# Fixed TensorE order and three runs of small matmuls per head pair, in a fused SSD and short-convolution layer

## Chip, cores and metric

One Trainium2 chip, one of its cores. The metric is the device time of one execution in microseconds (us), median of three runs: 1694.2 us for the kernel before (1693.04 to 1696.69).

## What is computed

One decoder layer over 2048 tokens with model width 1024, all in f32. The input is RMS-normalised and projected once (`h @ w_in`); two groups of heads read the projection, and their joint output goes through `w_out`, a second RMS norm, the residual, and a gated per-layer embedding. The change is in the first head group, 16 heads of 64 channels, a chunked state-space scan with chunks of 128 tokens:

```python
xd = (x * dt[..., None])                                   # per head, tokens x 64
cb = einsum("bclgn,bcsgn->bgcls", cc, bc)                  # C.B per chunk and B/C group
y_diag = einsum("bgrcls,bcsgrp->bclgrp", cb[:, :, None] * decay_in, xd)
states = einsum("bclgn,bclgrp->bcgrpn", bc, xd * decay_states[..., None])
...
y_off = einsum("bclgn,bcgrpn->bclgrp", cc, prev_states) * decay_out[..., None]
y = (y_diag + y_off) + d_skip[:, None] * x
...
yz = y_ssd * silu(z_ssd);  y_ssd = rmsnorm(yz, ssd_norm)   # RMS norm per B/C group
mix = concatenate([y_ssd, y_sc], -1) @ w_out
```

## The kernel before, in words

Channels lie on the 128 partitions, tokens along the free axis. Tokens come in two blocks `b` of 1024 (TB), eight chunks (NCH) each. A Winograd-like input projection (tiles `A_...`) fills the first 1038 us and leaves x, gates, masks' sums and so on in DRAM. Then comes the stage of the **heads**, then the output projection (`mo`) and the gate (`mg`).

In the heads' stage TensorE has two kinds of work. The large one is `os`, the short-convolution half of the output projection: `under()` (L807) yields 256 units of three 128x512 matmuls, 768 in all. The small one is the scan. Heads are handled in pairs of channel tiles `(j, j+4)`, gr 0 and gr 1, four pairs per block, eight pairs in all. For one pair, with the names that the trace shows:

- `loads` (L875): `xs`, one 128x1024 tile per gr, from `xs_d` in DRAM; three buffers.
- `transposes` (L879, "T0", "T1"): 8 transposes into a PSUM tile `px`, then VectorE makes `xd` = px times dt (L891, three buffers) and `xdd` = xd times a decay (L892).
- `decays` and `mask_load`/`mask`: the decay row `ea` (one buffer, exp on ScalarE at L902), and four masks `m` (four buffers, "m00" to "m11"), each one 512 KB broadcast load, 8 exponentials on ScalarE (L939) and one VectorE product with C.B (L942).
- `states` (L908): matmuls into `pst` (L912), then VectorE runs the recurrence over chunks into `sprev` (L926) and multiplies `ea` by C (L929).
- `offsets` (L944): matmuls of `sprev` and `ea` into two PSUM tiles `py` (L955), one per gr.
- `outputs` (L959, "out0", "out1"): matmuls of `xd` and the masks into the same `py` (L967), then on VectorE y (L970) and the gate (L971), written over `xs` and stored to `yz_d`; a square on ScalarE (L976) is summed into `ssum` by VectorE (L977).

`px`, `pst`, `py`, C.B (`pg`) and the norm's sums (`pn`, L230 in `inv_rms`) share three PSUM tiles of two banks (`pss`, L743). `os` uses two banks of its own, which ScalarE empties into `po` (L830).

A list `steps` (L1008 to L1022) names the parts in the order in which they are written, and after each step some `os` units are written, so that both are spread over each other. What TensorE in fact gets is not that order: a scheduler reorders instructions of an engine where data allow it, except for the few that `open_bank` (L217) ties together. An engine then executes its list strictly in order, and SyncE's DMA issues stand in such a list too.

Of the kernel before, what the change touches and what calls it, by code (L numbers as in the profile page):

```python
# [7 lines left out]
F32 = mybir.dt.float32  # L8
# [5 lines left out]
NOSYNC = mybir.DependencyInfo(mybir.DependencyClass.NoSync, mybir.DependencyReason.DATA)  # L14

P = 128
# [4 lines left out]
TB = 1024  # L21
# [5 lines left out]
NCH = TB // CH  # L27
# [33 lines left out]
def hybrid_kernel(ctx: ExitStack, tc: tile.TileContext, xT, pT, w_t, w_dt, w_o, w_g, w_p, cols_d, cst_d, outT):  # L61
    nc = tc.nc
    V, S, G, TE = nc.vector, nc.scalar, nc.gpsimd, nc.tensor
# [40 lines left out]
    def flat(ps):  # L104
        return ps.rearrange("p g t -> p (g t)")
# [4 lines left out]
    class Weights:  # L110
# [4 lines left out]
        def __init__(self, seq):  # L115
            self.seq, self.n, self.ready = seq, 0, []
# [9 lines left out]
        def next(self, held=0):  # L126

            self.fill(self.SLOTS - held)
            return self.ready.pop(0)
# [232 lines left out]
    with ExitStack() as st:  # L362
# [352 lines left out]
        for b, prs, order in groups:  # L715
# [16 lines left out]
            if b + 1 < NB:  # L732
# [5 lines left out]
                if n in (6, 7, 8, 9, 10):  # L738
                    next(prep, None)

    pss = ctx.enter_context(tc.tile_pool(name="pss", bufs=3, space=PSUM))  # L743
# [58 lines left out]
    with ExitStack() as st:  # L802
        t4 = st.enter_context(tc.tile_pool(name="t4", bufs=2))
# [31 lines left out]
        def heads(b):  # L835
# [34 lines left out]
            def pair(j):  # L870

                jts = (j, j + 4)
                xd, xdd, xs, gz, st = [None, None], [None, None], [None, None], [None, None], {}

                def loads(gr):  # L875
                    xs[gr] = t4.tile([P, TB], F32, tag="xs", name=f"xs_{b}{jts[gr]}", bufs=3)
                    nc.sync.dma_start(xs[gr], xs_d[b][jts[gr]])

                def transposes(gr):  # L879
                    jt = jts[gr]  # L880
                    px = flat(pss.tile([P, 2, TG], F32, tag="ssd", name=f"px_{b}{jt}"))
                    for c in range(NCH):
                        cs = slice(c * CH, (c + 1) * CH)
                        TE.transpose(px[:, cs], xs[gr][:, cs], ident)
                    xd[gr] = t4.tile([P, NCH, P], F32, tag="xd", name=f"xd_{b}{jt}", bufs=3)
                    xdd[gr] = t4.tile([P, NCH, P], F32, tag="xdd", name=f"xdd_{b}{jt}")

                    def bc(a):
                        return a[:, 2 * jt:2 * jt + 2, :].rearrange("p h c -> p c h").unsqueeze(3).to_broadcast([P, NCH, 2, 64])
                    r4 = lambda a: a.rearrange("p c (h q) -> p c h q", h=2)  # L890
                    V.tensor_tensor(r4(xd[gr]), px.rearrange("p (c h q) -> p c h q", c=NCH, h=2), bc(dts[b]), ALU.mult)  # L891
                    V.tensor_tensor(r4(xdd[gr]), r4(xd[gr]), bc(dst[b]), ALU.mult)  # L892
# [86 lines left out]
                def both(*fs):  # L979
                    return lambda: [f() for f in fs]  # L980

                ml = lambda *gh: lambda: mask_load(*gh)
                mk = lambda *gh: lambda: mask(*gh)
                return {"xs0": lambda: loads(0), "xs1": lambda: loads(1), "T0": lambda: transposes(0), "T1": lambda: transposes(1), "decays": decays,
                        "load0": both(decays_load, ml(0, 0), ml(0, 1)), "load1": both(ml(1, 0), ml(1, 1)),
                        "gz0": lambda: gates_load(0), "gz1": lambda: gates_load(1),
# [9 lines left out]
        steps = []  # L996
        no = lambda: None
        pairs, norms, begins, gs = [], [], [], []
        for b in range(NB):
# [5 lines left out]
        NJ = len(pairs) // NB  # L1005
        both = lambda *fs: lambda: [f() for f in fs]
        p = pairs[0]
        steps += [both(begins[0], p["xs0"], p["xs1"], p["load0"], p["load1"]), gs[0][0], gs[0][1], p["T0"],  # L1008
                  both(p["gz0"], p["gz1"]), p["decays"], p["T1"], no, p["m00"], no]
        for n, p in enumerate(pairs):  # L1010
            b, j = divmod(n, NJ)
            q = pairs[n + 1] if n + 1 < len(pairs) else dict.fromkeys(p, no)
            fresh = j == NJ - 1 and b + 1 < NB
            steps += [both(p["states"], q["xs0"]), p["m01"], p["m10"], p["m11"], p["offsets"], p["out0"]]
            steps += [both(q["load0"], begins[b + 1]) if fresh else q["load0"], q["T0"], both(q["decays"], q["xs1"])]
            if fresh:

                steps += [p["out1"], q["load1"], norms[b], gs[b + 1][0], gs[b + 1][1], both(q["T1"], q["gz0"], q["gz1"]), no,
                          q["m00"], no]
            else:  # L1020
                steps += [p["out1"], both(q["load1"], q["gz0"]), both(q["T1"], q["gz1"]), q["m00"], no]
        steps += [norms[-1]]  # L1022

        filler = under()
        units, lead = 0, 22
# [182 lines left out]
```

## Time and profile before

| | |
|---|---|
| median of the runs | 1694.2 us (1693.04 to 1696.69) |
| the profiled execution | 1696.41 us, its span 1694.7 us |
| TensorE busy | 1658.7 us, 98% of the span |
| VectorE, ScalarE, GpSimd busy | 1255.4, 783.5, 45.6 us |
| mean granted TensorE clock | 0.996 of full speed |
| DMA | 262.27 MB, mean 155 GB/s |

How to read it: one execution is profiled, and its time (1696.41 us) is 1.7 us above its span. The trace has two records for each f32 matmul of the scan (64 where the program lists 32 offsets; one each for `os`, `mo` and the transposes). Matmul records are pipelined, each starts before the one ahead has ended, so what a run of matmuls costs is read from its first start to the start of what follows. "Idle before" names what an engine waited for. A half granted clock (0.50) makes a matmul last twice as long.

### The profile page before, as it was taken

The numbers are of one execution on the slowest core, as the hardware profiler recorded it, in microseconds if no ns is written. First come the engines' busy times: TensorE is split into PE (matmuls) and PEld (weight loads), VectorE is DVE, ScalarE is ACT, GpSimd is POOL, SyncE is SP. The second block draws the span as 40 slices with busy tenths as digits, with TensorE's granted clock in tenths as the row PEclk, the third lists the DMA queues.
The fourth block names the chain that finished last, engine by engine and source line by source line (L and its number), as shares of the span: only waits on it lengthen the run. The fifth ranks groups of instructions, "written<-read, shape, count | busy, mean of one in ns | idle before, by whom it ended". The sixth has DMA issues, their size and how long they took to land.

```text
span 1694.7 us, 22635 instructions
## 1 busy us (share of the span) xinstructions
PE 1658.7 (98%) x8324; PEld 1351.9 (80%) x8324; DVE 1255.4 (74%) x1843; ACT 783.5 (46%) x1408; POOL 45.6 (3%) x79
## 2 busy tenths in 40 slices
PE   7999999999999999999999999999999899999998
PEld 5788888888888888888888888778777677788886
DVE  7997777988669867677777685689678748878632
ACT  7763444434337434343444353666575324252421
POOL 0000000000000100100000000000000000000000
PEclk9999999999999999999999999999999999999999
DMA  9462221773226322222222237789887735636422
GB/s 303 162 211 70 97 96 61 257 251 120 69 68 213 130 80 95 78 76 68 106 82 102 73 117 239 245 277 278 261 314 242 243 100 168 197 102 211 149 95 87
DMA packets 122691, 262.27 MB, mean 155 GB/s; under 512 B 17098, under 2 KB 19658, under 8 KB 121556
## 3 DMA queue, kind: packets, MB, share of 16 engines
q1 hardware_dynamic: 122580, 260.83, 46.4%
q8 instruction: 65, 1.06, 0.2%
q14 instruction: 46, 0.38, 0.1%
HBM read 192.45 MB, written 68.33 MB: 154 GB/s over the span
## 4 chain that ended last, share of the span: by engine, by line
PE 85%; DMA 6%; DVE 6%; ACT 2%; issue 1%; SPq 0%; DVEq 0%; ACTq 0%
PE mg L214 10%; PE mo L214 8%; PE os L826 6%; PE py L967 1%; PE A_xs1X L310 1%; PE A_gc6X L310 1%; PE A_gc7X L310 1%; PE A_gb6X L310 1%; PE A_z3X L310 1%; PE A_xs3X L310 1%; PE A_gc5X L310 1%; PE A_z2X L310 1%; PE A_xs2X L310 1%; PE A_gb4X L310 1%; PE A_gc4X L310 1%; PE A_gc3X L310 1%
## 5 line engine op out<-in xcount | busy, mean ns | idle before, releaser
L826 PE MATMUL os<-act_m,ws_os 128*128 128x512 f32 x768 | 186.0, 396 | 2.4 <-ACT po L830 1.7
L214 PE MATMUL mo<-act_m,ws_o 128*128 128x512 f32 x768 | 180.9, 396 | 4.3 <-DVE x L1060 4.3
L214 PEld LDWEIGHTS mo<-act_m,ws_o 128*128 128x128 f32 x768 | 144.1, 189 | 42.1 <-issue 6.1
L214 PE MATMUL mg<-act_x2s,ws_g 128*128 128x512 f32 x768 | 176.8, 391 | 0.7 <-ACT gth L1104 0.7
L826 PEld LDWEIGHTS os<-act_m,ws_os 128*128 128x128 f32 x768 | 141.2, 188 | 37.6 <-issue 6.6
L214 PEld LDWEIGHTS mg<-act_x2s,ws_g 128*128 128x128 f32 x768 | 143.0, 188 | 34.2 <-ACT gth L1104 4.4
L139 DVE TENSOR_TENSOR ws_A_gb<-wr_A_gb,ws_A_gb 128x512 fp32r<-128x512 f32 x96 | 65.8, 686 | 33.0 <-ACT ws_A_gb L138 32.9
L138 ACT CAST ws_A_gc<-wr_A_gc 128x512 fp32r<-128x512 f32 x96 | 59.7, 622 | 57.7 <-PE A_gc5X L310 8.3
L138 ACT CAST ws_A_gb<-wr_A_gb 128x512 fp32r<-128x512 f32 x96 | 59.7, 621 | 51.6 <-PE A_cb0Y L310 4.3
L604 DVE SCALAR_TENSOR_TENSOR xo<-ux,cols,xo 128x1024 f32<-128x1024 f32 x60 | 76.7, 1280 | 6.7 <-ACT xo L600 5.6
L939 ACT ACTIVATE m<-m,adt 128x128 f32<-128x128 f32 x256 | 77.5, 391 | 0.6 <-DMA m<-acs_d 0.5
L139 DVE TENSOR_TENSOR ws_A_gc<-wr_A_gc,ws_A_gc 128x512 fp32r<-128x512 f32 x96 | 66.0, 687 | 14.1 <-ACT ws_A_gc L138 12.8
L1105 DVE SCALAR_TENSOR_TENSOR gth<-gth,pe 128x512 f32<-128x512 f32 x32 | 22.1, 691 | 70.5 <-ACT gth L1104 70.4
L1104 ACT ACTIVATE gth<-mg 128x512 f32<-128x512 f32 x32 | 19.1, 598 | 103.7 <-PE mg L214 103.6
L214 PE MATMUL A_ple<-act_p,ws_p 128*128 128x512 f32 x192 | 48.2, 409 | 9.0 <-ACT ws_p L138 8.1
L942 DVE SCALAR_TENSOR_TENSOR m<-m,gsb 128x1024 f32<-128x1024 f32 x32 | 39.6, 1246 | 19.1 <-ACT m L939 16.8
L214 PEld LDWEIGHTS A_ple<-act_p,ws_p 128*128 128x128 f32 x192 | 37.4, 196 | 18.7 <-ACT ws_p L138 9.0
L139 DVE TENSOR_TENSOR ws_A_z<-wr_A_z,ws_A_z 128x512 fp32r<-128x512 f32 x48 | 32.9, 685 | 25.2 <-ACT ws_A_z L138 25.2
L203 ACT CAST act_m<-mraw 128x512 fp32r<-128x512 f32 x64 | 38.1, 621 | 28.9 <-DVE mraw L785 15.8
L138 ACT CAST ws_A_xs<-wr_A_xs 128x512 fp32r<-128x512 f32 x48 | 29.9, 623 | 44.3 <-issue 11.6
L138 ACT CAST ws_A_z<-wr_A_z 128x512 fp32r<-128x512 f32 x48 | 29.9, 623 | 41.9 <-DVE wr_A_z L187 8.6
L1060 DVE TENSOR_TENSOR x<-mo,part 128x512 f32<-128x512 f32 x32 | 22.0, 686 | 29.3 <-PE mo L214 29.3
(499 smaller groups left out, 3597.7 us busy)
## 6 DMA issues: line engine op xcount, KB each, us to landing
wr_A_gc<-in_w_t_dram SPq DMA_DIRECT2D x64, 256.0 KB, 2.5
wr_A_gb<-in_w_t_dram SPq DMA_DIRECT2D x64, 256.0 KB, 2.8
m<-acs_d SPq DMA_DIRECT2D x32, 512.0 KB, 7.7
ple_d<-A_pe SPq DMA_DIRECT2D x32, 256.0 KB, 5.1
wr_A_xs<-in_w_t_dram SPq DMA_DIRECT2D x32, 256.0 KB, 2.6
ysc_d<-vs SPq DMA_DIRECT2D x16, 512.0 KB, 2.7
wr_A_z<-in_w_t_dram SPq DMA_DIRECT2D x32, 256.0 KB, 3.0
xs_d<-xo SPq DMA_DIRECT2D x16, 512.0 KB, 4.0
```

Of the source, the lines that this page charges most:

```text
L138: S.copy(sp[:, 0, :kn, :], raw[:, :kn, :])
L139: V.tensor_tensor(sp[:, 1, :kn, :], raw[:, :kn, :], sp[:, 0, :kn, :].bitcast(F32), ALU.subtract)
L203: S.copy(a[:, 0, :], src)
L214: TE.matmul(out, sp[:, a, (k0 + k) % 4, :], act[k0 + k][:, b, :], start=k0 + k == 0 and q == 0, stop=k0 + k == n - 1 and q == 2)
L310: TE.matmul(out, sp[:, a, k % 4, :], t[:, b, ts_], start=p in OPENS and k == 0 and q == 0, stop=k == nk - 1 and q == 2, skip_group_check=True)
L604: V.scalar_tensor_tensor(o, u[:, q:q + TB], col(w0 + q), o, ALU.mult, ALU.add)
L826: TE.matmul(ps, sp[:, a, k, :], acts_o[tg][KD + kk][:, b_, :], start=kk == 0 and n == 0, stop=kk == KD - 1 and n == 2)
L939: S.activation(m[:, c, :], m[:, c, :], AF.Exp, bias=nacs[b][:, h, c:c + 1])
L942: V.scalar_tensor_tensor(mf, mf, 1.0, s["gsb"][gr], ALU.min, ALU.mult)
L1060: V.tensor_tensor(x2[d], ps[:, i, :], pt[:, i, :], ALU.add)
L1104: S.activation(th, ps, AF.Tanh, scale=0.5)
L1105: V.scalar_tensor_tensor(th, th, 1.0, pe, ALU.add, ALU.mult)
```

## The change

From the heads on, every TensorE instruction is tied to the one written before it (class `InOrder`, a dependency without a semaphore), so that TensorE executes them as they are written. The list of steps is written anew: out0 and out1 stand directly behind the offsets, T0 and T1 of the next pair stand together, both `xs` loads of the next pair stand at the pair's states, and at the end two empty steps stand ahead of the last norm. `xs` has four buffers in place of three, `xd` two (the pool's own number) in place of three. No operation is added or left out.

```diff
+    class InOrder:
+        def __init__(self, engine):
+            self.engine, self.last = engine, None
+        def __getattr__(self, name):
+            f = getattr(self.engine, name)
+            def call(*a, **k):
+                inst = f(*a, **k)
+                if self.last is not None:
+                    tc.add_manual_dep(inst.ins, self.last.ins.name, NOSYNC, reason="in the order of the trace")
+                self.last = inst
+                return inst
+            return call
+    TE = InOrder(TE)
...
-                    xs[gr] = t4.tile([P, TB], F32, tag="xs", name=f"xs_{b}{jts[gr]}", bufs=3)
+                    xs[gr] = t4.tile([P, TB], F32, tag="xs", name=f"xs_{b}{jts[gr]}", bufs=4)
...
-                    xd[gr] = t4.tile([P, NCH, P], F32, tag="xd", name=f"xd_{b}{jt}", bufs=3)
+                    xd[gr] = t4.tile([P, NCH, P], F32, tag="xd", name=f"xd_{b}{jt}")
...
-        steps += [both(begins[0], p["xs0"], p["xs1"], p["load0"], p["load1"]), gs[0][0], gs[0][1], p["T0"],
-                  both(p["gz0"], p["gz1"]), p["decays"], p["T1"], no, p["m00"], no]
+        steps += [both(begins[0], p["xs0"], p["xs1"], p["load0"], p["load1"]), gs[0][0], gs[0][1], both(p["T0"], p["T1"]),
+                  both(p["gz0"], p["gz1"]), p["decays"], p["m00"], no]
...
-            steps += [both(p["states"], q["xs0"]), p["m01"], p["m10"], p["m11"], p["offsets"], p["out0"]]
-            steps += [both(q["load0"], begins[b + 1]) if fresh else q["load0"], q["T0"], both(q["decays"], q["xs1"])]
+            steps += [both(p["states"], q["xs0"], q["xs1"]), p["m01"], p["m10"], p["m11"], no,
+                      both(p["offsets"], p["out0"], p["out1"]), both(q["load0"], begins[b + 1]) if fresh else q["load0"],
+                      both(q["T0"], q["T1"], q["decays"])]
             if fresh:
-                steps += [p["out1"], q["load1"], norms[b], gs[b + 1][0], gs[b + 1][1], both(q["T1"], q["gz0"], q["gz1"]), no,
-                          q["m00"], no]
+                steps += [q["load1"], norms[b], gs[b + 1][0], gs[b + 1][1], both(q["gz0"], q["gz1"]), q["m00"], no]
             else:
-                steps += [p["out1"], both(q["load1"], q["gz0"]), both(q["T1"], q["gz1"]), q["m00"], no]
-        steps += [norms[-1]]
+                steps += [both(q["load1"], q["gz0"]), q["gz1"], q["m00"], no, no]
+        steps += [no, no, norms[-1]]
```

The instructions' order at three places, as the built programs have it. In the changed kernel every TensorE instruction from the heads on carries the line of the helper, L751. Numbers behind a name are the tile's own.

**Place 1, TensorE, the offsets and outputs of the third pair of block 1.** Before, from the last `os` ahead of the offsets on:

```order
L826 MATMUL os_5_10892<-act_m_15_9963,ws_os_5_3_10604 128x512 x3
L955 MATMUL py_10796<-ea_10560,sprev_10724 64x128
L955 MATMUL py_10797<-ea_10560,sprev_10724 64x128
L884 MATMUL px_10876<-cst,xs_10742 128x128 x5
...
L967 MATMUL py_10796<-m_10563,xd_10582 64x128
...
L884 MATMUL px_10876<-cst,xs_10742 128x128 x3
L967 MATMUL py_10797<-m_10649,xd_10670 64x128
...
L826 MATMUL os_6_10965<-act_m_8_9641,ws_os_6_2_10609 128x512 x3
...
L884 MATMUL px_10944<-cst,xs_10897 128x128 x8
L912 MATMUL pst_11010<-xdd_10886,btok_9849 64x128
L826 MATMUL os_6_11167<-act_m_8_9899,ws_os_6_2_10609 128x512 x3
```

Changed, from the first output matmul of the same pair on (the offsets, 32 in a row, stand right ahead):

```order
L751 MATMUL py_10788<-m_10570,xd_10593 64x128
...
L751 MATMUL py_10789<-m_10617,xd_10606 64x128
...
L751 MATMUL os_4_10867<-act_m_8_9936,ws_os_4_2_10318 128x512 x3
...
L751 MATMUL px_10887<-cst,xs_10723 128x128 x8
L751 MATMUL px_10900<-cst,xs_10725 128x128 x8
L751 MATMUL os_4_10867<-act_m_12_9983,ws_os_4_3_10323 128x512 x3
```

The transposes of the next pair moved out of the offsets and outputs, and both sets stand together between `os` matmuls. A pair now reads: 16 px, 36 os, all pst, 30 os, all offsets, all outputs, 12 os.

**Place 2, TensorE, the end of the heads.** Before, the last `os`, the norm's sums (`pn`) and the first `mo`:

```order
L826 MATMUL os_7_11258<-act_m_15_9963,ws_os_7_3_10971 128x512 x3
L230 MATMUL pn_11280<-ssum_9850,ones_d 32x512 x2
L214 MATMUL mo_0_11327<-act_m_0_11181,ws_o_0_0_10976 128x512 x3
L230 MATMUL pn_11280<-ssum_9851,ones_d 32x512 x2
L214 MATMUL mo_0_11327<-act_m_1_11185,ws_o_0_0_10976 128x512 x3
```

Changed:

```order
L751 MATMUL os_7_11258<-act_m_13_9986,ws_os_7_3_11015 128x512 x3
L751 MATMUL pn_11277<-ssum_9870,ones_d 32x512 x2
L751 MATMUL pn_11277<-ssum_9871,ones_d 32x512 x2
L751 MATMUL os_7_11258<-act_m_14_10014,ws_os_7_3_11015 128x512 x3
L751 MATMUL os_7_11258<-act_m_15_10017,ws_os_7_3_11015 128x512 x3
L751 MATMUL mo_0_11327<-act_m_0_11202,ws_o_0_0_11020 128x512 x3
```

Before, three `os` matmuls stand between the last output matmul and the sums; now 60 do, and six more behind them.

**Place 3, VectorE, from the first y of one pair to the states of the next** (second to third pair of block 1), in the changed kernel, where L990, L991, L997, L911, L912, L962, L946, L949 and L805 are L970, L971, L977, L891, L892, L942, L926, L929 and L785 of before:

```order
L990 SCALAR_TENSOR_TENSOR xs_10119<-xs_10119,ds_101,py_10485 128x1024
...
L991 TENSOR_TENSOR xs_10119<-xs_10119,gz_10338 128x1024
L990 SCALAR_TENSOR_TENSOR xs_10121<-xs_10121,ds_101,py_10486 128x1024
...
L997 TENSOR_TENSOR ssum_9870<-ssum_9870,gz_10338 128x1024
L991 TENSOR_TENSOR xs_10121<-xs_10121,gz_10346 128x1024
L911 TENSOR_TENSOR xd_10593<-px_10584,dts_105 128x1024
L911 TENSOR_TENSOR xd_10606<-px_10597,dts_105 128x1024
L912 TENSOR_TENSOR xdd_10594<-xd_10593,dst_109 128x1024
L997 TENSOR_TENSOR ssum_9871<-ssum_9871,gz_10346 128x1024
L912 TENSOR_TENSOR xdd_10607<-xd_10606,dst_109 128x1024
L962 SCALAR_TENSOR_TENSOR m_10570<-m_10570,gsb_9867 128x1024
...
L949 SCALAR_TENSOR_TENSOR ea_10567<-ct_9863,ea_10567 128x1024 x2
```

Before, L891 and L892 of gr 0 stand between L970 and L971, and those of gr 1 behind the first mask. Now both outputs' work stands ahead of both transposes'. Left out here are two mraw products (L805), and ahead of the last row three weight splits (L139), one L805 and the 14 steps of `sprev`.

## Rows read from the trace of the kernel before

**Rows 1.** The page: the chain that ended last, by engine.
```profile
PE 85%; DMA 6%; DVE 6%; ACT 2%; issue 1%; SPq 0%; DVEq 0%; ACTq 0%
```

**Rows 2.** TensorE's waits, 1035 to 1360 us: total us, times, longest us.
```profile
PE pn L230 <- DVE ssum L977: 4.7, 2, 3.8
PE px L884 <- DMA xs<-xs_d: 3.8, 2, 2.2
...
PE os L826 <- ACT po L830: 1.7, 1, 1.7
PE px L884 <- DVE m L942: 0.9, 2, 0.5
```

**Rows 3.** TensorE's timeline, third pair of block 1: start, us, instruction, count, idle before.
```profile
1264.61 1.03 PE L884 MATMUL px<-cst,xs 128*128 128x128 f32 x8
1265.58 0.43 PE L912 MATMUL pst<-xdd,btok 128*64 128x128 f32 x2
1265.94 3.92 PE L826 MATMUL os<-act_m,ws_os 128*128 128x512 f32 x16
1269.79 1.96 PE L912 MATMUL pst<-xdd,btok 128*64 128x128 f32 x30
1271.68 5.28 PE L826 MATMUL os<-act_m,ws_os 128*128 128x512 f32 x22
1276.89 0.44 PE L955 MATMUL py<-ea,sprev 64*64 64x128 f32 x4
1277.26 0.77 PE L884 MATMUL px<-cst,xs 128*128 128x128 f32 x5
1277.95 1.96 PE L955 MATMUL py<-ea,sprev 64*64 64x128 f32 x60
1279.85 1.97 PE L967 MATMUL py<-m,xd 128*64 128x128 f32 x32
1281.75 0.55 PE L884 MATMUL px<-cst,xs 128*128 128x128 f32 x3
1282.22 1.97 PE L967 MATMUL py<-m,xd 128*64 128x128 f32 x32
1284.12 11.17 PE L826 MATMUL os<-act_m,ws_os 128*128 128x512 f32 x48
1296.83 1.06 PE L884 MATMUL px<-cst,xs 128*128 128x128 f32 x8 [1.53 <-DMA xs<-xs_d]
```

**Rows 4.** TensorE's timeline, end of the heads and start of the output projection.
```profile
1313.19 3.71 PE L967 MATMUL py<-m,xd 128*64 128x128 f32 x64
1316.83 0.96 PE L826 MATMUL os<-act_m,ws_os 128*128 128x512 f32 x3
1321.61 1.05 PE L230 MATMUL pn<-ssum,ones_d 128*32 128x512 f32 x4 [3.81 <-DVE ssum L977]
1322.59 1.49 PE L214 MATMUL mo<-act_m,ws_o 128*128 128x512 f32 x3
1325.01 1.92 PE L230 MATMUL pn<-ssum,ones_d 128*32 128x512 f32 x4 [0.92 <-DVE ssum L977]
1326.86 29.57 PE L214 MATMUL mo<-act_m,ws_o 128*128 128x512 f32 x122
```

**Rows 5.** Busy by stretch: length, five engines' busy us, granted clock, DMA share, GB/s.
```profile
1322.80:1329.60 6.80, 5.88 (x14) 2.82 (x14) 5.57 (x9) 2.52 (x4) 0.00 (x0) 0.50 0.58 193
1329.60:1333.00 3.40, 3.40 (x16) 2.83 (x15) 2.48 (x4) 1.25 (x2) 0.00 (x0) 1.00 0.68 208
```

**Rows 6.** VectorE's timeline in the pair of rows 3.
```profile
1271.86 2.77 DVE L926 SCALAR_TENSOR_TENSOR sprev<-sprev,ea,pst 128x64 f32<-128x64 f32 x14 [0.92 <-PE pst L912]
1274.55 2.35 DVE L929 SCALAR_TENSOR_TENSOR ea<-ct,ea 128x1024 f32<-128x1024 f32 x2
...
1281.89 1.28 DVE L970 SCALAR_TENSOR_TENSOR xs<-xs,ds,py 128x1024 f32<-128x1024 f32 x1 [2.05 <-PE py L967]
```

**Rows 7.** The masks `m`: time from DMA issue to landing, 1040 to 1330 us.
```profile
DMA to landing us min/median/max: 6.9/7.7/8.5
```

## The prediction

> **What bounds the kernel now.** I read the chain that ended last first, then TensorE's own waits, then TensorE's order of time in the heads' stage. The chain is TensorE for 85% of the span [rows 1], so time is to be had only where TensorE is idle, slow, or spends more than its work needs. The waits say where it is idle around the heads: 4.7 us for the norm's sums, 3.8 us at two transposes for a load of `xs`, 1.7 us once for an emptied `os` bank, 0.9 us at transposes behind a mask product [rows 2]. The order of time of one pair shows the third kind: the scan's small matmuls stand in nine pieces between `os` runs, and a piece that is cut costs more than the whole [rows 3]. The end of the stage shows the second: after an idle stretch of 3.81 us and shorter ones [rows 4] the granted clock is 0.50, which is 1.2 of 2.4 GHz, for the 6.8 us up to 1329.6 us, and full after it [rows 5].
>
> **Fewer pieces: 1.1 us per pair.** All costs are from one start to the next. Transposes: before in pieces of 8, 5 and 3, which take 0.97, 0.69 and 0.47 us, 2.13 together [rows 3]. The slope is (0.97 - 0.47)/5 = 0.10 each, so one piece of 16 costs 1.60 to 1.77 us (0.97 + 8 x 0.10): 0.36 to 0.53 saved. States: 0.36 + 1.89 us in two pieces [rows 3], in one 1.89 and two more at 1.89/30 = 0.06, so 2.02: 0.23 saved. Offsets: 0.37 + 1.90 us [rows 3], in one 1.90 + 4 x 0.032 = 2.03: 0.24 saved. Outputs: twice 1.90 us with transposes between [rows 3], but 3.64 us where both stand together (1313.19 to 1316.83 us) [rows 4]: 0.16 saved. That is 0.99 to 1.16 us, and I take 1.1. The `os` runs of a pair were three (16, 22, 48) [rows 3] and are three again (36, 30, 12), so what entering and leaving them costs stays. Eight pairs give **8.8 us**. The first pairs are cut in other places, and the boundary of the blocks differs, so the bounds are 7 and 10.
>
> **Waits that go: 4.7 us.** The two waits for `xs` (3.8 us [rows 2]; the one of 1.53 us stands in [rows 3]) come from three buffers: the pair's second tile needs the tile whose result has just been stored, so the load waits for the store to land. With four buffers the next pair's loads go into the tiles of the pair before this one, stored a whole pair earlier, and they are issued at the states, before 30 `os`, offsets, outputs and 12 `os`. That also takes a blocked issue off SyncE's queue, on which the masks stand. The 0.9 us behind mask products [rows 2] go too, since both transposes now stand ahead of the masks. The 1.7 us for the `os` bank [rows 2] I leave where they are: that is the first pair, where ScalarE makes masks in the same order; the upper bound of the gain takes them in. `xd` with two buffers costs nothing: the outputs that read the old ones stand ahead of the transposes in TensorE's fixed order, 12 `os` matmuls away.
>
> **The end: 8.0 us.** Between 1316.83 and 1326.86 us, 10.03 us, TensorE does three `os`, three `mo` and two pieces of `pn` [rows 4]. An `os` matmul costs 0.233 us (48 of them from 1284.12 us to 1295.30 us, which is 1296.83 less the idle 1.53) [rows 3], the first `pn` piece 0.98 us (1321.61 to 1322.59) [rows 4]. The work is 6 x 0.233 + 2 x 0.98 = 3.4 us, so 6.6 are lost. From there to 1329.6 us another 2.74 us run at half clock [rows 5], 1.4 lost. Now 60 `os` matmuls, 60 x 0.233 = 14.0 us, stand between the last output and the sums. The second sum was ready 8.2 us after the last output had ended (1325.01 - 1316.83) [rows 4], so it is covered by 5.8 us, there is no idle stretch and no fall of the clock. Without that cover it would cost what it costs now.
>
> **What it adds.** At the boundary of the blocks the first norm's sums stand behind 12 `os`, 16 transposes and 12 `os`: 2 x 2.8 + 1.7 = 7.3 us after the last output. By the end's 8.2 us [rows 4] that is 0.9 us too early; and VectorE has two weight splits and both `xd` products ahead of the second sum there. I bound it by 0.8 and 4 us (the longest idle of this kind, 3.81 [rows 4]) and take **2.0**, nearer to the row of the same operation. Behind the waiting `pn`, TensorE's fixed order holds C.B of block 1, and with it the masks of that pair.
>
> **Does a pair fit?** In the changed order the states stand 12 `os`, 16 px and 36 `os` behind the last output: 2.8 + 1.7 + 8.4 = 12.9 us. VectorE's list by then has two each of y, gate, sum, `xd` and `xdd`, ten products of 128x1024. One takes 1.17 us (2.35/2 [rows 6]), ten 11.7, two mraw products half as wide 1.2 more. It starts when out0 is done, 1.8 us before the last output's end, so it is done at 11.1: 1.8 us of slack. Offsets stand 2.0 + 7.0 us further, at 21.9; `sprev` and `ea` follow the states (14.9) with 2.77 + 2.35 us [rows 6], done at 20.1: again 1.8. Masks' loads land within 8.5 us [rows 7]; the first is queued behind the store of gr 0 on SyncE, at about 0.5, so it is there at 9 at the latest, and wanted at 11. So a pair should not wait; for pairs with more splits I add **1.5 us** in all, between 0 and 12 (1.5 each).
>
> The Trainium skill speaks against the change here: "TensorEngine Tiling (Array Packing)", section PSUM Bottleneck, says that small tiles speed up TensorE but not the emptying of PSUM, which can become the bound. The row decides for the trace so far: VectorE stood 2.05 us idle for `py` before emptying it [rows 6], not TensorE for VectorE. If that page were right for the changed order, the first rival below would be the result.
>
> **Sum.** 8.8 + 4.7 + 8.0 = 21.5, less 2.0 and 1.5: 18.0 us. From the profiled execution's own 1696.4 us that gives 1678.4; it lies 2.2 us above the median of the runs (1694.2), so I forecast **1676 us**.
>
> **Rivals.** (1) VectorE becomes the bound of each pair. Against: 1.8 us of slack twice. For: a pair's list is 16 products at 1.17, 2.8 for `sprev` and some six splits or mraw products at 0.6, 25 us of a pair of 12.9 + 9.0 + 5.7 = 27.6 us; four more half-width operations ahead of the states overrun the slack. Then each pair gives back 1.5 us, 12 in all: 1688 us. (2) The end's gain does not stay: `mo` starts sooner after the norm, and its later operands hang on that norm, so the idle 3.81 + 0.92 us [rows 4] turns up inside `mo`: 1681 us. (3) The other side: TensorE, tied to the written order, stands at the offsets, since VectorE's list has the first mask ahead of `sprev`, and that mask's load stands on SyncE behind a store that waits for VectorE's gate. TensorE has nothing else to turn to. It decides from 18.0/8 = 2.25 us per pair on. A wait as long as the 3.81 us [rows 4] is followed by 6.8 us of half clock [rows 5], 3.4 us more: in four of the eight pairs 4 x 7.2 = 29 us, 1705 us. Against: loads of 7.7 us [rows 7] with slack behind them.
>
> **How the numbers follow.** Forecast 0.70; rival 1 0.14; rival 2 0.08; rival 3 0.08. Bounds of the first: most, 10 + 4.7 + 1.7 + 8.0 - 0.8 = 23.6 us, 1670.6; least is near rival 1. The range 1669 to 1689 holds the forecast, rival 2 and most of rival 1, and leaves out rival 3 and the ends. A change of 0.2%, 3.4 us, is about what a measurement can tell from none. Faster 0.88 (forecast, rival 2, most of rival 1), within 0.2% 0.04 (the weak end of rival 1), slower 0.08.
>
> **What would show it.** Right: a pair's period near 27.6 us without idle marks on px, pst or the offsets; no wait of px for `xs`; no 0.50 stretch of clock near the start of `mo`; `pn` at the end without idle, at the boundary with 1 to 4 us. Wrong: waits of pst or the offsets for `xdd`, `sprev` or `ea` that come back in every pair (rival 1 or 3, told apart by whether VectorE was busy or waited for a mask), or a longer wait of `mo` for VectorE's x (rival 2). If pieces cost less than rows 3 suggest, the period shows it with no idle at all.

## The result: 1% slower, with a gain in the heads near the forecast

The changed kernel takes 1714.7 us (median of 5 runs, 1711.42 to 1716.55); the kernel before, run beside it, 1696.0 us (1693.04 to 1704.17). The ratio is 1.0099, 95% interval 1.0081 to 1.0117. The forecast of 1676.0 us and its range are missed, on the other side of no change. The profiled execution of the changed kernel took 1711.4 us, its span is 1709.7 us (before 1694.7). One run of experiment 9, 2395.54 us at a mean granted clock of 0.655, is left out of its figures.

The 15.0 us between the spans fall in two parts of opposite sign. The first `os` starts 0.7 us earlier than before (1037.56 against 1038.29 us). From there to the first `mo` it is 272.8 us against 284.3, so 11.5 are gained, although before still had 0.92 us of idle and half of the norm's sums to come at that point [rows 4]. From the start of the first `mo` to the start of the last `mg` matmul it is 393.5 us against 366.2, so 27.3 are lost. -0.7 - 11.5 + 27.3 = 15.1.

**The heads after.** TensorE's timeline from one pair's offsets to the next pair's (start, us, instruction, count, idle before), which answers to [rows 3]:

```profile
1077.88 1.98 PE L751 MATMUL py<-ea,sprev 64*64 64x128 f32 x64
1079.78 3.72 PE L751 MATMUL py<-m,xd 128*64 128x128 f32 x64
1083.43 3.02 PE L751 MATMUL os<-act_m,ws_os 128*128 128x512 f32 x12
1086.29 1.91 PE L751 MATMUL px<-cst,xs 128*128 128x128 f32 x16
1087.95 8.43 PE L751 MATMUL os<-act_m,ws_os 128*128 128x512 f32 x36
1096.32 1.97 PE L751 MATMUL pst<-xdd,btok 128*64 128x128 f32 x32
1098.21 7.09 PE L751 MATMUL os<-act_m,ws_os 128*128 128x512 f32 x30
1105.24 1.98 PE L751 MATMUL py<-ea,sprev 64*64 64x128 f32 x64
```

No row has an idle mark, and the period is 1105.24 - 1077.88 = 27.36 us (forecast 27.6). TensorE's waits from 1035 to 1360 us, beside [rows 2]:

```profile
PE mo L751 <- DVE x L1081: 9.5, 3, 7.9
PE py L751 <- DVE m L962: 2.3, 1, 2.3
PE pst L751 <- DVE xdd L912: 1.8, 1, 1.8
PE pg L751 <- DMA bt<-cb_d: 1.4, 1, 1.4
PE px L751 <- DVE xs L990: 1.4, 1, 1.4
PE os L751 <- ACT po L850: 0.8, 1, 0.8
```

The waits for `xs` loads and for the norm's sums are gone; four others of 1.4 to 2.3 us came once each; and the largest line is new: `mo` waits for VectorE's x.

**The end of the heads and the output projection after**, the same view, beside [rows 4]:

```profile
1293.99 13.91 PE L751 MATMUL os<-act_m,ws_os 128*128 128x512 f32 x60
1307.83 1.06 PE L751 MATMUL pn<-ssum,ones_d 128*32 128x512 f32 x8
1308.83 1.66 PE L751 MATMUL os<-act_m,ws_os 128*128 128x512 f32 x6
1310.32 5.61 PE L751 MATMUL mo<-act_m,ws_o 128*128 128x512 f32 x24
1323.80 13.36 PE L751 MATMUL mo<-act_m,ws_o 128*128 128x512 f32 x48 [7.88 <-DVE x L1081]
1337.95 11.21 PE L751 MATMUL mo<-act_m,ws_o 128*128 128x512 f32 x48 [0.78 <-DVE x L1081]
...
1556.11 11.17 PE L751 MATMUL mg<-act_x2s,ws_g 128*128 128x512 f32 x48 [0.69 <-ACT gth L1125]
1567.97 11.17 PE L751 MATMUL mg<-act_x2s,ws_g 128*128 128x512 f32 x48 [0.69 <-ACT gth L1125]
```

The norm's sums run without idle, and `mo` starts. But 24 matmuls later TensorE stands 7.88 us, and from then on it stands 0.7 to 1.6 us before nearly every 48 matmuls, to the end of the kernel. `x` is VectorE's sum of a finished `mo` bank and its part from DRAM, `gth` is ScalarE's reading of a finished `mg` bank. The waits of the whole stretch, in the changed kernel from 1300 us on:

```profile
PE mo L751 <- DVE x L1081: 21.3, 15, 7.9
PE mg L751 <- ACT gth L1125: 9.6, 14, 0.7
```

and in the kernel before from 1315 us on (beside the 4.7 us at `pn` [rows 2]):

```profile
PE mo L214 <- DVE x L1060: 4.3, 4, 1.7
PE mg L214 <- ACT gth L1104: 0.7, 1, 0.7
```

So 30.9 us in 29 waits against 5.0 in 5. A wait costs more than its mark: in `mg`, 48 matmuls with one mark of 0.69 take 1567.97 - 1556.11 = 11.86 us, where before 672 `mg` in one run took 153.84 us, 10.99 per 48. That is 0.87 per wait, 0.18 above the mark, and if the waits in `mo` cost the same above theirs, 24 more waits make 4.3 us. The long wait is also followed by half clock, as in [rows 5] (busy by stretch; the column ahead of the last two is the granted clock):

```profile
1318.20:1329.00 10.80, 5.20 (x13) 4.19 (x14) 7.65 (x13) 5.31 (x8) 0.00 (x0) 0.53 0.92 287
1329.00:1333.00 4.00, 4.00 (x19) 3.28 (x19) 0.69 (x1) 0.51 (x1) 0.00 (x0) 1.00 0.91 325
```

13 matmuls took 5.2 us in place of 3.0, 2.2 lost, against 1.4 in the stretch of [rows 5]. Together 25.9 + 4.3 + 0.8 = 31.0 us. The 27.3 above plus the 3.6 us by which before's first three `mo` stand ahead of the rest (4.27 less 0.7 of work [rows 4]) is 30.9, so the loss is accounted for, with the 4.3 us as an estimate.

**What the fixed order took away.** `mo` and `mg` fill PSUM tiles of two banks: 24 matmuls for one bank (a unit), 24 for the other, then the next tile. In the written order both banks of a tile follow each other. The built programs, TensorE, from the 24th `mo` on, before and changed (the number in `mo_0_11327` is the tile's own, `ws_o_1_0` is the weight of the tile's second bank):

```
before:
MATMUL mo_0_11327<-act_m_7_11249,ws_o_0_1_10981 128x512 x3
MATMUL mo_0_11432<-act_m_0_11316,ws_o_0_0_10976 128x512 x3
...
MATMUL mo_2_11491<-act_m_3_11201,ws_o_2_0_11340 128x512 x2
MATMUL mo_0_11327<-act_m_0_11181,ws_o_1_0_11330 128x512 x3
changed:
MATMUL mo_0_11327<-act_m_7_11249,ws_o_0_1_11025 128x512 x3
MATMUL mo_0_11327<-act_m_0_11202,ws_o_1_0_11330 128x512 x3
```

Before, the scheduler had put 27 matmuls of the next tiles between the first bank's end and the second bank's start, and a few, mostly four, at later places. In both built programs the second bank's first matmul has a wait for the reader of the first bank; four matmuls take 0.9 us, about as long as most of the marks. In the changed order nothing stands between, and the second bank's first matmul waits until VectorE (x, L1081) or ScalarE (gth, L1125) has read the first bank. The last `mg` rows above show it: the matmuls end at 1567.28 us (1556.11 + 11.17), the next starts at 1567.97, and in between stands

```profile
1567.32 0.60 ACT L1125 ACTIVATE gth<-mg 128x512 f32<-128x512 f32 x1 [4.33 <-PE mg L751]
```

The Trainium skill, "Perfetto Trace Analysis", section Matmuls, advises that independent groups rotate through different PSUM banks, so that emptying one overlaps the next group's matmuls. The trace here narrows that: the two units did use different banks, and TensorE still waited 0.69 us each time, since both banks belong to one tile (experiment 2).

### The profile page after: what moved, and what is told of

It is laid out like the page before. It is cut to its first block, busy times and chain, and to the rows that moved or that the text cites. A ratio compares the mean times of both kernels' runs of the same rounds, so it can differ in the third digit from the quotient of the medians.

```text
span 1709.7 us, 22654 instructions
## 1 busy us (share of the span) xinstructions
PE 1652.3 (97%) x8324; PEld 1352.4 (79%) x8324; DVE 1254.9 (73%) x1843; ACT 782.9 (46%) x1408; POOL 47.5 (3%) x79
## 4 chain that ended last, share of the span: by engine, by line
PE 83%; DVE 7%; DMA 5%; ACT 2%; issue 2%; SPq 0%; DVEq 0%; ACTq 0%
PE mg L751 10%; PE mo L751 8%; PE os L751 6%; DMA mraw<-yz_d 2%; PE py L751 2%; PE A_xs1X L310 1%; PE A_gc6X L310 1%; PE A_gb7X L310 1%; PE A_gb6X L310 1%; PE A_gc2X L310 1%; PE A_cb0X L310 1%; PE A_gc7X L310 1%; PE A_xs3X L310 1%; PE A_gc5X L310 1%; PE A_z2X L310 1%
## 5 line engine op out<-in xcount | busy, mean ns | idle before, releaser
L751 PE MATMUL mo<-act_m,ws_o 128*128 128x512 f32 x768 | 181.0, 395 | 21.3 <-DVE x L1081 21.3
L751 PEld LDWEIGHTS mo<-act_m,ws_o 128*128 128x128 f32 x768 | 144.7, 190 | 58.3 <-DVE x L1081 20.4
L751 PE MATMUL mg<-act_x2s,ws_g 128*128 128x512 f32 x768 | 179.0, 392 | 9.6 <-ACT gth L1125 9.6
L751 PE MATMUL os<-act_m,ws_os 128*128 128x512 f32 x768 | 184.3, 396 | 1.5 <-ACT po L850 0.8
L751 PEld LDWEIGHTS mg<-act_x2s,ws_g 128*128 128x128 f32 x768 | 143.0, 188 | 45.9 <-ACT gth L1125 16.8
L751 PEld LDWEIGHTS os<-act_m,ws_os 128*128 128x128 f32 x768 | 142.5, 189 | 35.6 <-issue 4.4
L139 DVE TENSOR_TENSOR ws_A_gb<-wr_A_gb,ws_A_gb 128x512 fp32r<-128x512 f32 x96 | 65.8, 686 | 33.2 <-ACT ws_A_gb L138 33.1
L139 DVE TENSOR_TENSOR ws_A_gc<-wr_A_gc,ws_A_gc 128x512 fp32r<-128x512 f32 x96 | 65.9, 687 | 14.2 <-ACT ws_A_gc L138 13.2
L1125 ACT ACTIVATE gth<-mg 128x512 f32<-128x512 f32 x32 | 19.1, 598 | 109.6 <-PE mg L751 109.5
L1081 DVE TENSOR_TENSOR x<-mo,part 128x512 f32<-128x512 f32 x32 | 22.0, 689 | 46.6 <-PE mo L751 45.6
L139 DVE TENSOR_TENSOR ws_A_z<-wr_A_z,ws_A_z 128x512 fp32r<-128x512 f32 x48 | 32.9, 686 | 25.2 <-ACT ws_A_z L138 25.2
L962 DVE SCALAR_TENSOR_TENSOR m<-m,gsb 128x1024 f32<-128x1024 f32 x32 | 39.0, 1244 | 15.5 <-ACT m L959 13.7
```

Of the source, the lines that this page charges most:

```text
L139: V.tensor_tensor(sp[:, 1, :kn, :], raw[:, :kn, :], sp[:, 0, :kn, :].bitcast(F32), ALU.subtract)
L751: inst = f(*a, **k)
L962: V.scalar_tensor_tensor(mf, mf, 1.0, s["gsb"][gr], ALU.min, ALU.mult)
L1081: V.tensor_tensor(x2[d], ps[:, i, :], pt[:, i, :], ALU.add)
L1125: S.activation(th, ps, AF.Tanh, scale=0.5)
```

## Experiments

**Theory 1:** the loss is the order that is fixed beyond the heads; two units sharing a tile wait for each other when nothing stands between them. **Theory 2:** the loss is what the heads hand over: `mo` starts right behind the norm, with late loads (rival 2 of the prediction, larger). Two further questions were which part of the change brings the heads' gain, and whether its terms were sized right. Ratios are to runs of the kernel before on the same chip, so ratios are compared, not medians.

### 1. Fixed order in the heads alone

```diff
+    TE = TE.engine
     with ExitStack() as st:
         pp = st.enter_context(tc.tile_pool(name="pp", bufs=2))
```

> The change, but TensorE's order is fixed in the heads alone; from the output projection (mo) on it is the scheduler's again. Theory 1 (the fixed order takes away the interleaving of the two banks of one PSUM tile in mo and mg): the short waits of 0.7 to 0.9 us before every 48th mo and mg go, mg's idle falls from 9.6 us to under 1.5, mo's from 21.3 to under 9; the heads' gain of some 16 us stays. The first x is still late, so up to 3.4 us of the 7.9 us at the start of mo may stay: 1683 us (1678 to 1688), ratio to before about 0.992. Theory 2 (the loss comes from mo starting right behind the norm and its late loads, whatever the order): the start of mo stalls about 8 us as now and later waits stay: 1700 us or more.

Measured: 1684.0 us, ratio 0.9915 (0.9891 to 0.9939), as theory 1 has it. TensorE's waits from 1310 us on:

```profile
PE mo L214 <- DVE x L1083: 2.9, 4, 1.6
PE mo L214 <- DVE act_m L204: 1.0, 2, 0.8
PE mo L214 <- ACT act_m L203: 0.9, 2, 0.6
PE mg L214 <- ACT gth L1127: 0.7, 1, 0.7
```

With the heads as in the change, 30.9 us of waits become 5.5. Theory 2 falls as the main cause; 1.9 us of waits for the operands of the second token group are what is left of it.

### 2. The same order, one tile per unit

```diff
-                    ps = pss.tile([P, 2, TG], F32, tag="ssd", name=f"mo_{tg}_{dp}")
                     pt = L3.get("part", tg, dp)
                     for i in range(2):
+                        ps = pss.tile([P, 2, TG], F32, tag="ssd", name=f"mo_{tg}_{dp + i}")
...
-                            mm3([(ps[:, i, :], sp[2 * i + q], acts_o[tg])], 4 * q, 4, KD)
+                            mm3([(ps[:, 0, :], sp[2 * i + q], acts_o[tg])], 4 * q, 4, KD)
```

(and the same in `gate`)

> The change with its fixed order everywhere, but each unit of 24 mo or mg matmuls takes a PSUM tile of its own (of which it uses one bank), in place of two units sharing the two banks of one tile. The order of the matmuls is the same as in the change. Theory 1 (the second bank of a tile waits until the first has been emptied, since both belong to one tile): the waits before every 48th matmul go, mg's idle falls from 9.6 us to under 1.5 us, the 7.9 us at the start of mo shrink to under 4 (operands of the second token group come next): 1681 us (1677 to 1688). If instead the order itself, or the emptying of PSUM as such, is what costs: mg's waits of 0.69 us stay and the time stays within 4 us of 1715.

Measured: 1680.1 us, ratio 0.9888 (0.9866 to 0.9910). TensorE's waits from 1310 us on, and its last run of `mg`:

```profile
PE mo L751 <- DVE act_m L204: 3.3, 6, 0.8
PE mo L751 <- ACT act_m L203: 1.1, 2, 0.6
```

```profile
1514.24 158.34 PE L751 MATMUL mg<-act_x2s,ws_g 128*128 128x512 f32 x696
```

The matmuls of `mo` and `mg` stand in the same order as in the change, and no wait for x or gth is left: 696 `mg` run without a mark. What costs is neither the order by itself nor the emptying of PSUM, but that both banks are one tile when the order puts them side by side.

### 3. Before, with the order fixed from `mo` on

The class of the change, applied behind the heads:

```diff
+    TE = InOrder(TE)
     with ExitStack() as st:
         pp = st.enter_context(tc.tile_pool(name="pp", bufs=2))
```

> The kernel before, heads untouched, but TensorE's order fixed from the output projection on. Theory 1: the loss shows alone: 14 waits of 0.69 us in mg, some 13 of 0.8 to 0.9 us in mo, and a longer one at its start: 1718 us (1712 to 1728). Theory 2 (the loss belongs to what the heads hand over to mo): within 4 us of before, 1692 to 1700.

Measured: 1728.7 us, ratio 1.0181 (1.0155 to 1.0208): with the old heads the loss stands without the gain, some 31 us. Waits from 1324 us on:

```profile
PE mo L1046 <- DVE x L1080: 20.2, 15, 5.0
PE mg L1046 <- ACT gth L1124: 9.6, 14, 0.7
PE pn L230 <- DVE ssum L977: 6.8, 1, 6.8
```

The 14 waits in `mg` are the same to a tenth. The time is just over the expected range. The profiled span is 32.3 us above that of before (1727.0 against 1694.7); 28.4 of them lie behind the first `mo`, and ahead of it the norm's sums wait 6.8 us, where before 3.8 stood ahead of it [rows 4].

### 4. An earlier load for the first x

```diff
         L3 = Loads(st, "pl3", 3)
+        L3.begin("part", 0, 0)
```

> The change as it is, but the load of the first part tile (the sum that the first x needs) is begun ahead of the mixes' loads, in place of when the first mo unit is written. If the 7.9 us ahead of the 25th mo come from that load, which was issued 8 us after the norm behind a blocked issue of a mix load: the wait shrinks to under 4 us and the stretch at half clock behind it with it, the other waits stay: 1708 us (1703 to 1712). If they come from VectorE's queue or the norm's chain: within 3 us of the change, 1712 to 1718.

Measured: 1713.0 us, ratio 1.0085 (1.0063 to 1.0106); the long wait is 8.2 us. The edit did not do what it was for: SyncE still issued the load only at 1320.42 us, 8.7 us behind the first `mo` (in the change 7.8). VectorE's timeline shows what stood ahead of x:

```profile
1323.21 1.41 DVE L805 SCALAR_TENSOR_TENSOR mraw<-mraw,cols,gn 128x512 f32<-128x512 f32 x2 [0.56 <-DMA mraw<-yz_d]
1324.76 0.69 DVE L1082 TENSOR_TENSOR x<-mo,part 128x512 f32<-128x512 f32 x1
```

Here x has no idle mark: it stands in VectorE's list behind products of the second token group's operands, which wait for their loads. In the change x waited for its own load:

```profile
1323.06 0.69 DVE L1081 TENSOR_TENSOR x<-mo,part 128x512 f32<-128x512 f32 x1 [0.77 <-DMA part<-part_d]
```

There VectorE reached x at 1322.29 us, 6.4 us after the first 24 `mo` had ended (1310.32 + 5.61 = 1315.93). So an earlier load could have taken 0.8 us at most off the wait of 7.9; the rest is the place of x in VectorE's list. That is read from the two traces; no run moved x in that list. Experiments 1 and 2 show that the wait costs nothing like 7.9 us when TensorE has other work there.

### 5. The new steps and buffers without a fixed order

```diff
-    TE = InOrder(TE)
```

> The new list of steps and the new buffers, with no fixed order at all. In the built program the scheduler keeps the scan in the same three runs per pair as the fixed order does (16 px, all pst, offsets and outputs together), only the boundary of the blocks differs by a few pieces. If the written steps and buffers bring the heads' gain: as the run with the order fixed in the heads alone, within 4 us, about 1683 us (1678 to 1689). If the fixed order brings it: nearer to before, 1690 us or more.

Measured: 1678.2 us, ratio 0.9891 (0.9867 to 0.9914), from the first `os` to the first `mo` 270.6 us. Waits in the heads:

```profile
PE py L974 <- DVE ea L948: 1.8, 4, 0.6
PE py L986 <- DVE m L961: 1.7, 1, 1.7
PE os L845 <- ACT po L849: 1.5, 1, 1.5
PE pn L230 <- DVE ssum L996: 0.8, 1, 0.8
```

The fixed order, the first part of the change, brings none of the gain: without it the scheduler keeps the new runs.

### 6 and 7. Steps and buffers apart

The new steps without a fixed order, with the old buffers:

```diff
-                    xs[gr] = t4.tile([P, TB], F32, tag="xs", name=f"xs_{b}{jts[gr]}", bufs=4)
+                    xs[gr] = t4.tile([P, TB], F32, tag="xs", name=f"xs_{b}{jts[gr]}", bufs=3)
...
-                    xd[gr] = t4.tile([P, NCH, P], F32, tag="xd", name=f"xd_{b}{jt}")
+                    xd[gr] = t4.tile([P, NCH, P], F32, tag="xd", name=f"xd_{b}{jt}", bufs=3)
```

> The new list of steps without a fixed order, as in the run before, but with the old buffers (three xs, three xd). In the built program the scheduler then cuts the scan as before: transposes 8 and 8 or between the offsets, states 1 and 15 (of 16), offsets 2 and 62, and 24 os in place of 66 between the last outputs and the output projection. If xd with two buffers is what keeps the pieces whole, and pieces cost what the prediction took (1.1 us per pair), most of the gain goes: 8 us for pieces, 4 for waits for xs, some 3 at the end: 1692 us (1687 to 1697). If pieces cost next to nothing: 1683 us or less.

Measured: 1700.1 us, ratio 1.0009 (0.9989 to 1.0029): no gain at all. TensorE's timeline, the later part of a pair:

```profile
1241.34 0.43 PE L974 MATMUL py<-ea,sprev 64*64 64x128 f32 x4
1241.71 0.66 PE L903 MATMUL px<-cst,xs 128*128 128x128 f32 x4
1242.29 1.96 PE L974 MATMUL py<-ea,sprev 64*64 64x128 f32 x60
...
1247.83 0.66 PE L903 MATMUL px<-cst,xs 128*128 128x128 f32 x4
...
1260.91 1.06 PE L903 MATMUL px<-cst,xs 128*128 128x128 f32 x8 [1.95 <-DMA xs<-xs_d]
```

The pieces and the wait for `xs` are back as in [rows 3], whatever the steps say. In the built program, three `xs` with two `xd` give exactly the same order as three and three, so it is the fourth `xs` that decides, not `xd` as the expectation had it. (Four `xs` with three `xd` has no run: they don't fit beside each other.)

The kernel before with the new buffers alone:

```diff
-                    xs[gr] = t4.tile([P, TB], F32, tag="xs", name=f"xs_{b}{jts[gr]}", bufs=3)
+                    xs[gr] = t4.tile([P, TB], F32, tag="xs", name=f"xs_{b}{jts[gr]}", bufs=4)
...
-                    xd[gr] = t4.tile([P, NCH, P], F32, tag="xd", name=f"xd_{b}{jt}", bufs=3)
+                    xd[gr] = t4.tile([P, NCH, P], F32, tag="xd", name=f"xd_{b}{jt}")
```

> The kernel before with the new buffers alone (four xs, two xd), the old list of steps, no fixed order. In the built program the scheduler now leaves 30 os behind the last outputs ahead of the last norm (before: 3), transposes stand in two runs of 8, states and offsets are cut less. By the prediction's terms: waits for xs go (4 to 5 us), the end gains most of its 8 us, pieces little: 1687 us (1682 to 1692). If buffers alone do nothing: 1694 us or more.

Measured: 1686.7 us, ratio 0.9935 (0.9913 to 0.9956), as expected; no wait for `xs` is left, and 0.2 us at `pn`. Its timeline still has 58 pieces of the scan (16 runs of px, 10 of pst, 16 of offsets, 16 of outputs), that of experiment 5 has 33 (8, 8, 9, 8). With about the same idle in the heads (5.6 and 5.8 us) and a granted clock of 1.00 throughout, they take 278.4 us against 270.6 from the first `os` to the first `mo`: 7.8 us for 25 pieces, 0.31 each, with the `os` runs that they cut included. So the steps do bring their gain once the fourth `xs` is there.

### 8. New steps, no fixed order, one tile per unit

Experiment 5 with the edit of experiment 2.

> The new list of steps and new buffers without a fixed order, and each unit of mo and mg with a PSUM tile of its own. If the remaining waits of mo for x (2.8 us) and of mg (0.7 us) come from two units sharing a tile, they go: 2 to 4 us less than the run without a fixed order, 1675 us (1672 to 1679), if the late second norm does not make mo wait for its operands instead; then the same within 2 us.

Measured: 1674.9 us, ratio 0.9866 (0.9843 to 0.9888), the lowest of all; the waits for x and gth are gone, 3.9 us for operands came. Its interval overlaps those of experiments 2 and 5. That the fixed order costs some 4 us in the heads is pointed to, not settled: the ratios differ by 0.0022 (this run against 2) and 0.0024 (5 against 1). In the traces the heads, from the first `os` to the first `mo`, take 270.6 and 271.8 us without the fixed order (5 and 8), and 272.8, 277.1 and 274.6 with it (the change, 1 and 2), so kernels with the same heads differ by 4.3 us among themselves.

### 9. Before, one tile per unit

> The kernel before with nothing changed but that each unit of mo and mg takes a PSUM tile of its own. Before, the scheduler's order hides most of the sharing; what is left are 4.3 us of mo's waits for x and 0.7 us in mg. If these come from the sharing of a tile too: they go, and some waits for operands of the second token group (1 to 4 us, as in the run of the change with one tile per unit) may come: 1695 us where before gives 1699 (ratio 0.996 to 1.000). If the sharing matters in a fixed order alone: ratio 1.000 within 0.002, waits unchanged.

Measured: 1690.4 us, ratio 0.9961 (0.9947 to 0.9975). The 5.0 us of waits for x and gth go and 2.1 for operands come: sharing a tile cost a little in the scheduler's order as well. These waits are 2.9 of the 6 to 7 us that the ratio says; the rest was not traced.

### 10. The cover at the end taken away

```diff
-        steps += [no, no, norms[-1]]
+        steps += [norms[-1]]
```

on experiment 2, with the empty steps of the last pair left out.

> The change with one PSUM tile per unit, but the empty steps behind the last outputs are taken out, so that 18 os matmuls in place of 60 stand between the last outputs and the last norm (the other 42 are spread over the pairs). By the prediction's term for the end, the second sum is ready 8.2 us after the last output, 18 os cover 4.2: some 4 us of idle at pn and 1.5 to 3.5 us of a stretch at half clock behind it come back: 1686 us (1683 to 1690), where the version with 60 os took 1680. If the cover at the end is worth nothing: 1680 within 2.

Measured: 1694.6 us, ratio 0.9985 (0.9968 to 1.0001). That is 0.0097 above experiment 2, some 16 us where 6 were expected. TensorE's timeline:

```profile
1309.82 4.37 PE L751 MATMUL os<-act_m,ws_os 128*128 128x512 f32 x18
1321.51 1.92 PE L751 MATMUL pn<-ssum,ones_d 128*32 128x512 f32 x4 [7.32 <-DVE ssum L997]
1325.03 1.92 PE L751 MATMUL pn<-ssum,ones_d 128*32 128x512 f32 x4 [1.59 <-DVE ssum L997]
```

The second sum came 1325.03 - 1309.82 = 15.2 us after the last output, not 8.2: VectorE's list had operand products for `mo` between y, gate and sum. There were 8.9 us of idle, and from 1319.6 us on 10.2 us at a granted clock of 0.51. Between the last output and the first `mo` (1329.60 us) stand 19.8 us, of which 24 `os` and the sums need 7.5 at full clock, so 12.2 are lost at the end, where the prediction had 8.0. The run does not give the price of the cover alone: the 42 `os` went into the pairs, and there two waits are longer than in experiment 2 (3.8 against 0.7 us at `px` for VectorE's y, 3.0 against 1.2 at the boundary's `pn`).

## Why the prediction was wrong, step by step

- **Fewer pieces, 8.8 us: right, undersized.** A pair took 30.69 us before without its last wait, with 86 `os` [rows 3]; less 8 `os` at 0.2325 that is 28.83, against 27.36 now: 1.47 per pair, where 1.1 stood. The transposes take 1.66 us, the states 1.89, the offsets 1.90, the outputs 3.65. The states and the offsets in one run take no longer than their larger pieces did before (1.89 and 1.90), where the prediction added 0.13 to each.
- **Waits that go, 4.7 us: right.** Neither the wait for `xs` nor that for a mask at `px` is left, and the `os` bank's is 0.8 in place of 1.7 (1.5 and 3.6 in experiments 1 and 2).
- **`xs`: right, and incomplete.** The prediction used the fourth `xs` for an earlier load only. Experiments 5 to 7 show that the order in which the scheduler places the scan hangs on it too: the new steps bring nothing without it.
- **The end, 8.0 us: right.** No idle at `pn`, full clock at the first `mo`. Experiment 10 shows that without it 12.2 us are lost there.
- **The boundary's norm, 2.0 us: came out without a mark in the change**; its sums take 0.6 us more than those at the end. In experiments 2 and 10, with the same order there, it was 1.2 and 3.0 us, inside the bounds.
- **Does a pair fit, 1.5 us: undersized.** The four waits of 1.4 to 2.3 us make 6.9. Rival 1 had the place but not the reason. At the first, outputs that wait for a mask at 1166.97 us, VectorE's list had the mask product behind operand products that waited 1.37 us for ScalarE. The second is a load for C.B. Ahead of the third and fourth (`px` at 1240.34 us, `pst` at 1251.92) VectorE stood idle, with y queued behind a product whose load was late:

```profile
1238.34 0.75 DVE L805 SCALAR_TENSOR_TENSOR mraw<-mraw,cols,gn 128x512 f32<-128x512 f32 x1 [4.93 <-DMA mraw<-yz_d]
1239.01 1.27 DVE L990 SCALAR_TENSOR_TENSOR xs<-xs,ds,py 128x1024 f32<-128x1024 f32 x1
```

  So the rule on emptying PSUM that the prediction weighed from the Trainium skill ("TensorEngine Tiling (Array Packing)", section PSUM Bottleneck) did not become the result: 4.93 us of idle stand ahead of the emptying, not a full VectorE. Nor is it the result in `mo` and `mg`: with a tile per unit the same engines empty as many banks, and TensorE waits for none of them (experiment 2).
- **The sum: here it failed.** For the heads alone it holds: 287.9 us from the first `os` to `mo` at work before (1326.86 - 1038.29, less 0.7 for three `mo`) against 272.8, 15.1 gained, where the forecast's 18.0 less its 1.4 for the half clock is 16.6. That the two lie so near is in part luck. Against their terms the pieces gave 3.0 us more (eight pairs at 1.47 would make 11.8), the boundary 1.4 and the `os` bank 0.9 more; the waits took 5.4 more (6.9 in place of 1.5), and a stretch at a lower clock behind one of them (last section) some 1.5. But the sum ends at the first `mo`. The front matter says that every TensorE instruction from the heads on is tied; the prediction gave that no term behind the heads, neither a cost nor a reason for none. That term is -31 us. Where one tile per unit takes it away, the ratio is 0.9888 (experiment 2); the forecast was 0.9893 of 1694.2.
- **Rival 2 named the place, but neither the size nor the cause.** It saw idle "inside `mo`", 4.7 us, and ascribed it to the norm. Its sign, a longer wait of `mo` for VectorE's x, came. In the change 21.3 us stand in `mo` and 9.6 in `mg`, where no rival looked; experiment 1 removes them without moving the norm. **Rival 3** forecast a slower kernel for another reason, which did not come in that size: the one wait of the outputs for a mask is 2.3 us.

What in the views of before could have shown it: waits of 4.3 us in `mo` and 0.7 in `mg` over 32 tiles say only that the order then in place hides the emptying of PSUM. Whether the written order hides it too is read from the two built programs, at the `mo` rows quoted above.

## What to carry to other kernels

A change that fixes an engine's order from some point on is costed to the last instruction that it ties: compare the two orders in every stage behind that point, and ask at each place where the scheduler had put something between a producer and its next use what will cover that wait now. Two units that follow each other in a fixed order take PSUM tiles of their own, or other matmuls between them. Before fixing an order, try whether a missing buffer is what lets the scheduler leave it: here, with the new list of steps, a fourth `xs` did the whole work of the tie.

## What had not been expected of the hardware

- An idle mark of 0.69 us between two runs of 128x512 matmuls costs 0.87 us from start to start (11.86 against 10.99 us per 48 before), 0.94 by the pace of experiment 2 (158.34 us for 696, 10.92 per 48).
- One idle stretch of 2.3 us ahead of a pair's outputs (1166.97 us) was followed by 3.4 us at a granted clock of 0.55 in the mean, close to the lower level of 0.50, 1.2 GHz:

```profile
1168.40:1171.80 3.40, 3.40 (x16) 2.64 (x13) 3.40 (x5) 1.06 (x1) 0.00 (x0) 0.55 0.66 183
```

- The 28 short waits of 0.7 to 1.6 us in `mo` and `mg` had no such stretch behind them: the granted clock is 1.00 from 1337.9 to 1514 us and 0.99 from there to the end.
